# Chunk inputs in two tiles, decays loaded first, gate rows a product ahead, and a chunk's finish in a later step: one layer of a hybrid decoder on one core

## The chip, the core and the metric

The kernel runs on one core of a Trainium2 chip. The time is the device time of one execution in microseconds (us), from start to end, as the median of several runs. A trace of one further, profiled execution goes with it. The core has five engines with their own instruction streams: PE (TensorE, matmuls and transposes; PEld is its weight load), DVE (VectorE), ACT (ScalarE), POOL (GpSimd) and SP (SyncE, which here only issues DMA transfers; some are issued by ACT). The engines meet through semaphores. The granted clock is the share of full speed at which TensorE was allowed to run.

## What is computed

One layer: a pooling branch P and a state-space branch S run in parallel, are gated, added and multiplied by `w_o`. Prompt: 1 sequence of 1024 rows; sample: 8 sequences of 8 rows (64 rows, so 1088 in all). Cut to what matters here:

```python
u_pool, z_pool, z_ssm, xbc, dt_raw, g_raw = split(h @ w_in)
p = (pool_mix(u_pool) * silu(z_pool)) @ w_pool_out            # 512 -> 1024
xs, B, C = split(silu(causal_conv(xbc)))                      # 2048, 4*128, 4*128
# ssd, per chunk of 128 rows and per group g of 8 heads:
acs = cumsum(dt * A); decay = exp(where(mask, acs_i - acs_j, -inf))
y = ((C B^T) * decay * dt) @ x + (C * exp(acs)) @ h
h = h * exp(acs_last) + (B^T, exp(acs_last - acs) * dt) @ x
y = rmsnorm((y + d_skip * x) * silu(z_ssm), ssm_norm_g)
s = y @ w_ssm_out                                             # 2048 -> 1024
x = x + gate * ((sigmoid(g_p) * p + sigmoid(g_s) * s) @ w_o)
```

Outputs are the final norm of both streams and the new pool, convolution and ssm states.

## The kernel before

Each matrix operand is held as a high and a low part, and a product takes three matmuls (high by high, high by low, low by high), in helpers whose lines are L359, L360 and L361 or L608, L609 and L610. Channels lie on the partitions and rows run along the free axis.

**Three stages** can be told apart in time. To about 815 us the conditioning and the in-projection run; they leave x, B and C of the four groups (`xbc_d[g]`, six blocks of 128 channels: four of x, one of B, one of C), `silu(z)` (`z_d[g]`) and the gate rows (`gp_d`, `gs_d`) in DRAM. From 815 to 1127 us comes the **chunk stage**, which the change edits. The rest, to 1307 us, is the last group's share of the S product, the gating, the product with `w_o` and the final norm.

**The chunk stage** walks 32 chunks, 4 groups `g` of 8 chunks `c` with 128 rows each, and lays the large products between them so that PE has work while a chunk's small steps run on the other engines. `chunk(g, c)` is a generator of steps:

- step 1 loads `xb` (x, B and C of the chunk, 128x6x128, L1492, 4 buffers) and `dec` (the cumulated decays spread over partitions, 128x8x128, L1187 in `decays`, 3 buffers);
- step 2 makes `cE` from `dec` on ACT (L1499), masks `dec` on POOL (L1192) and takes its 8 exponentials on ACT (L1201, one for a head);
- step 3 loads `sz` (the chunk of `silu(z)`, L1505, 3 buffers), transposes x and B on PE (L1508, L1510) and multiplies C by B (L1511); ACT copies B and C out (L1513, L1515); DVE scales x into `xd`, `xw` (L1519, L1521) and multiplies `dec` and `cE` (L1526, L1528);
- step 4 is the matmuls `pu` (L1533) and `inner` (L1213, L1216), the new state `hn` (POOL L1539, DVE L1541) and `v`, the output with the skip term, written over x in `xb` (DVE L1546). Then follows `finish`: `v*sz` (DVE L1468), the high part `yh` (ACT L1470), the square into `sz` (ACT L1471), the low part `yl` (POOL L1472), and the sum of squares into `sq_acc` (POOL L1473 to L1479);
- for the last chunk of a group, step 5 transposes the state out through `fo` (1 buffer, L1552 to L1555).

`sample_end(g)` does the same finish for the sample's 64 rows; it takes a tile of the ring `sz` and loads it (L1483), and `v` (L1485).

**The main loop** (L1803 to L1825) runs in iteration `i`: a step of `wos`; step 3 of chunk i+1; products; step 5 of chunk i-1 if there is one; a step of `wos`; step 4 with the finish of chunk i; the sample's loads where i%8 is 2, its finish where i%8 is 4; step 1 of chunk i+3; step 2 of chunk i+2; products. `products` advances the large products at RATE 2.56 blocks an iteration: first eight P products (`P_unit`), each with a gate row `R` (128x1088) loaded from `gp_d` as it begins (L1719), multiplied by DVE (L1722) and stored by ACT (L1724); then the S products of groups 0 to 2. The weights of a product are loaded two products ahead (L459, L460). `wos` splits `w_o` into high and low parts in 16 pieces: a piece is loaded (`pw`, 2 buffers, L1772), copied to its high part on ACT (L1775), which is stored, and POOL subtracts (L1777); in its next step the low part is written back through SP (L1781).

`in_line` (L1830) puts PE's and SP's instructions in the order in which the program is written; the scheduler orders ACT, DVE and POOL, and `behind(...)` is a hint to it that holds a piece of work behind other work on an engine. SP takes its queue in order: an issue that waits for a buffer holds all issues behind it.

Of the kernel before, what the change touches and what calls it, by code (L numbers as in the profile page):

```python
# [8 lines left out]
F32 = mybir.dt.float32  # L9
# [11 lines left out]
P = 128  # L21
# [4 lines left out]
NS = 64  # L26
# [7 lines left out]
NC = SEQ // CH  # L34
# [12 lines left out]
def tile_pool_ssd_step(  # L47
# [9 lines left out]
    def nm(s):  # L57
        uid[0] += 1
        return f"{s}_{uid[0]}"
# [31 lines left out]
    def R(shape=(P, T), dt=F32):  # L91
        return hs.tile(list(shape), dt, tag="R", name=nm("R"), bufs=3)
# [17 lines left out]
    load = nc.sync.dma_start  # L110
    store_ = nc.scalar.dma_start
# [1072 lines left out]
    def decays(dec, g, c):  # L1184

        S = P if c < NC else NS
        load(dec, acs_d[c, 8 * g:8 * g + 8, :S].partition_broadcast(S))  # L1187
# [273 lines left out]
    CKL = ("sz", "v")  # L1461

    def ckt(shape, tag, bufs=2):
        return (cl if tag in CKL else ca if tag in ("dec", "xb", "cE") else ck).tile(list(shape), F32, tag=tag, name=nm(tag), bufs=bufs)

    def finish(g, o, S, v, sz):

        V.tensor_tensor(v, v, sz, ALU.mult)  # L1468
        yhc = yh[g][:, :, o:o + S]
        act(yhc, v, AF.Copy)  # L1470
        act(sz, v, AF.Square)  # L1471
        nc.gpsimd.tensor_tensor(yl[g][:, :, o:o + S], v, yhc.bitcast(F32), ALU.subtract)  # L1472
        nc.gpsimd.tensor_tensor(sz[:, 0:2], sz[:, 0:2], sz[:, 2:4], ALU.add)  # L1473
        sa = sq_acc[:, o:o + S]
        if g == 0:
            nc.gpsimd.tensor_tensor(sa, sz[:, 0], sz[:, 1], ALU.add)
# [12 lines left out]
    def chunk(g, c):  # L1489
        o = c * P  # L1490
        xb = ckt([P, 6, P], "xb", 4)
        load(xb, xbc_d[g][:, :, o:o + P])  # L1492
        Bf, Cf = xb[:, 4], xb[:, 5]
        dec = ckt([P, 8, P], "dec", 3)
        decays(dec, g, c)
        yield
        if c > 0:
            cE = ckt([P, 8, P], "cE")
            act(cE, dec, AF.Exp, scale=-1.0)  # L1499
# [5 lines left out]
        load(sz, z_d[g][:, :, o:o + P])  # L1505
        px = PB()
        for q in range(4):
            nc.tensor.transpose(px[:, q * P:(q + 1) * P], xb[:, q], ident)  # L1508
        pbc = PB()
        nc.tensor.transpose(pbc[:, :P], Bf, ident)  # L1510
        mm(pbc[:, P:2 * P], Bf, Cf, start=True, stop=True)  # L1511
        bt = ckt([P, P], "bt", 2)
        act(bt, pbc[:, :P], AF.Copy)  # L1513
        if c > 0:
            act(pbc[:, 2 * P:3 * P], Cf, AF.Copy)  # L1515
        pxv = px.rearrange("p (h d) -> p h d", d=64)
        heads = slice(8 * g, 8 * g + 8)
        xd = ckt([P, 8, 64], "xd", 2)
        V.tensor_tensor(xd, pxv, dtT[:, c, heads].unsqueeze(2).to_broadcast([P, 8, 64]), ALU.mult)  # L1519
        xw = ckt([P, 8, 64], "xw", 1)  # L1520
        V.tensor_tensor(xw, pxv, wdT[:, c, heads].unsqueeze(2).to_broadcast([P, 8, 64]), ALU.mult)  # L1521
        if g == c == 0:
            yield
            far(dec, c)
            exps(dec, g, c)
        V.tensor_tensor(dec, dec, pbc[:, P:2 * P].unsqueeze(1).to_broadcast([P, 8, P]), ALU.mult)  # L1526
        if c > 0:
            V.tensor_tensor(cE, cE, pbc[:, 2 * P:3 * P].unsqueeze(1).to_broadcast([P, 8, P]), ALU.mult)  # L1528
        yield
        if c == 0:  # L1530
            yh[g], yl[g] = [Y4(hs if g % 2 else hp) for _ in range(2)]
        pu = PC()
        mm(pu, bt, xw.rearrange("p h d -> p (h d)"), start=True, stop=True)  # L1533
        pi = inner(xd, dec, P, *((hst[g], cE) if c > 0 else ()))
        hn = ckt([P, 512], "hst", 2)
        if c == 0:
            act(hn, pu, AF.Copy)
        else:
            nc.gpsimd.tensor_tensor(hn.rearrange("p (h d) -> p h d", d=64), hst[g].rearrange("p (h d) -> p h d", d=64),  # L1539
                                    Elb[:, c, heads].unsqueeze(2).to_broadcast([P, 8, 64]), ALU.mult)  # L1540
            V.tensor_tensor(hn, hn, pu, ALU.add)  # L1541
        hst[g] = hn

        v = xb[:, 0:4]
        for q in range(4):
            V.scalar_tensor_tensor(v[:, q], v[:, q], Dv[:, 4 * g + q:4 * g + q + 1], pi[:, q], ALU.mult, ALU.add)  # L1546
        finish(g, o, P, v, sz)
        if c == NC - 1:
            yield
            pt = PB()  # L1550
            for q in range(4):
                nc.tensor.transpose(pt[:, q * P:(q + 1) * P], hn[:, q * P:(q + 1) * P], ident)  # L1552
            fo = ckt([P, 4, P], "fo", 1)
            act(fo, pt.rearrange("p (q n) -> p q n", n=P), AF.Copy)
            store_(new_ssm_p[0, 0, 8 * g:8 * g + 8].rearrange("(q h) p n -> (h p) q n", h=2), fo)  # L1555

# [154 lines left out]

    def P_unit(m):
        def run(w):
            if m == 0:
                sg = first_g[0]
            else:
                sg = R()
                with behind(mybir.EngineType.SP):
                    load(sg, gp_d[m])  # L1719

            def done(o, n, ps):
                V.tensor_tensor(sg[:, o:o + n], ps[:, :n], sg[:, o:o + n], ALU.mult)  # L1722
# [43 lines left out]

    def wo_splits():
        raws = {}
        for n in range(18):
            if n < 16:  # L1770
                raws[n] = ck.tile([P, 512], F32, tag="pw", name=nm("pw"), bufs=2)
                load(raws[n], w_o[0, n // 2 * P:n // 2 * P + P, n % 2 * 512:n % 2 * 512 + 512])  # L1772
            if 0 < n < 17:
                hi = ck.tile([P, 512], F32R, tag="ph", name=nm("ph"), bufs=1)
                act(hi, raws[n - 1], AF.Copy)  # L1775
                store_(wo_d[(n - 1) // 2][:, 0, (n - 1) % 2 * 512:(n - 1) % 2 * 512 + 512], hi.bitcast(F32))
                nc.gpsimd.tensor_tensor(raws[n - 1].bitcast(F32R), raws[n - 1], hi.bitcast(F32), ALU.subtract)  # L1777
                lo = raws.pop(n - 1)
            yield
            if 0 < n < 17:  # L1780
                load(wo_d[(n - 1) // 2][:, 1, (n - 1) % 2 * 512:(n - 1) % 2 * 512 + 512], lo)  # L1781
            yield
    wos = wo_splits()
    RATE = 2.56
# [2 lines left out]
    def products(t):  # L1787

        nonlocal made
        while made < RATE * t:  # L1790
            next(pc_, None)
            made += 1

    first_engines = (mybir.EngineType.PE, mybir.EngineType.Activation, mybir.EngineType.DVE, mybir.EngineType.SP)
    in_line(first_engines, True)
    next(seq[0])
# [3 lines left out]
    next(seq[1])  # L1800
    next(pc_)
    in_line(first_engines)
    for i in range(len(seq)):  # L1803
# [12 lines left out]
        if i % NC == 2:  # L1816
            ends = sample_end(i // NC)
            next(ends)
        if i % NC == 4:
            next(ends, None)  # L1820
        if i + 3 < len(seq):
            next(seq[i + 3])
        if i + 2 < len(seq):
            next(seq[i + 2])
        products(i + 1.0)  # L1825
    next(seq[-1], None)
    for it in (pc_, wos):
        for _ in it:
            pass
    in_line((mybir.EngineType.PE, mybir.EngineType.SP))  # L1830
    right.__exit__(None, None, None)
    while right_all:
        right_all.pop().__exit__(None, None, None)
# [223 lines left out]
```

## Time and profile before

| | us |
|---|---|
| median of 3 runs | 1303.44 |
| lowest and highest run | 1301.71, 1304.66 |
| the profiled execution's own time | 1308.79 |
| its span, first to last instruction | 1307.1 |

The mean granted clock of the profiled execution is 0.99. In 40 slices of the span (32.7 us each), a digit is the busy share of a slice in tenths; PEclk is the granted clock in tenths:

```profile
PE   7999999999999999999999999989999999999998
DVE  4685778866978688776666764666767767466433
PEclk9999999999999999999999999989999999999999
```

The chunk stage is slices 26 to 35. PE is busy nearly throughout; one slice, the 27th, about 850 to 882 us, has PE and its clock lower.

### The profile page before, as it was taken

What the parts mean: (1) busy time and instruction counts of PE and PEld (TensorE: products, weight loads), DVE (VectorE), ACT (ScalarE), POOL (GpSimd) and SP (SyncE); (2) the same over time, 40 slices, a digit from 0 to 9 for tenths busy, and PEclk for the clock granted to TensorE, in tenths of its full rate; (3) what the DMA queues carried; (4) which work ended last, traced back from release to release, by engine and by line L of the source; (5) the groups of instructions that cost most, each with busy time, mean ns of one, the idle gap of its engine ahead of it and who ended that gap; (6) DMA issues with size and microseconds to landing.
All of it is one profiled execution on the core that took longest, in us unless ns stands there. A gap on an engine that the chain in (4) does not pass through costs nothing.

```text
span 1307.1 us, 26274 instructions
## 1 busy us (share of the span) xinstructions
PE 1263.8 (97%) x9739; PEld 1174.2 (90%) x9739; DVE 899.7 (69%) x1608; ACT 662.5 (51%) x1528; POOL 669.5 (51%) x563
## 2 busy tenths in 40 slices
PE   7999999999999999999999999989999999999998
PEld 6779999999999999999999999978898788999786
DVE  4685778866978688776666764666767767466433
ACT  5665357375656564546556544545776555201211
POOL 1007668676869676665534435244676757314000
PEclk9999999999999999999999999989999999999999
DMA  9737345464455544445565656977778778575631
GB/s 333 245 110 228 112 147 184 146 204 150 153 166 197 167 152 132 160 133 143 161 206 170 180 169 221 303 248 268 226 243 271 246 244 283 198 262 158 227 101 52
DMA packets 232257, 251.68 MB, mean 193 GB/s; under 512 B 29217, under 2 KB 176369, under 8 KB 232122
## 3 DMA queue, kind: packets, MB, share of 16 engines
q1 hardware_dynamic: 160032, 171.60, 41.3%
q10 hardware_dynamic: 72098, 78.41, 17.6%
q8 instruction: 77, 1.26, 0.4%
q14 instruction: 50, 0.41, 0.1%
HBM read 167.06 MB, written 83.01 MB: 191 GB/s over the span
## 4 chain that ended last, share of the span: by engine, by line
PE 58%; issue 8%; DMA 8%; POOL 6%; DVE 4%; ACT 2%; SPq 0%; ACTq 0%; POOLq 0%; DVEq 0%
PE ps L608 6%; PE ps L609 6%; PE ps L610 6%; PE mm L608 6%; PE mm L610 6%; PE mm L609 5%; PE mm L359 3%; PE mm L360 3%; PE mm L361 3%; PE ps L2004 2%; PE ps L2003 2%; PE ps L2005 2%; PE ps L1213 2%; POOL G L1912 2%; DMA dec<-acs_d 1%
## 5 line engine op out<-in xcount | busy, mean ns | idle before, releaser
L168 POOL TENSOR_TENSOR wlo<-rawA,whi 128x512 fp32r<-128x512 f32 x120 | 179.4, 1499 | 179.6 <-ACT whi L165 104.0
L168 POOL TENSOR_TENSOR wlo<-raw,whi 128x512 fp32r<-128x512 f32 x92 | 149.9, 1636 | 122.1 <-ACT whi L165 87.5
L359 PE MATMUL mm<-Y,whi 128*128 128x352 f32 (+1 forms) x480 | 165.8, 345 | 5.6 <-DVE R L1722 4.8
L360 PE MATMUL mm<-Y,whi 128*128 128x352 f32 (+1 forms) x480 | 159.5, 332 | 0.3 <-DVE Y L1570 0.3
L361 PE MATMUL mm<-Y,wlo 128*128 128x352 f32 (+1 forms) x480 | 159.0, 331 | 0.0
L608 PE MATMUL mm<-Y,whi 128*128 128x272 f32 x496 | 146.4, 295 | 0.6 <-DVE GA L624 0.5
L610 PE MATMUL mm<-Y,wlo 128*128 128x272 f32 x496 | 144.4, 291 | 2.6 <-POOL wlo L168 2.1
L608 PE MATMUL ps<-Y,whi 128*128 128x272 f32 x496 | 144.0, 290 | 2.6 <-ACT o L808 2.2
L609 PE MATMUL ps<-Y,whi 128*128 128x272 f32 x496 | 143.6, 290 | 0.0
L610 PE MATMUL ps<-Y,wlo 128*128 128x272 f32 x496 | 143.1, 289 | 0.0
L609 PE MATMUL mm<-Y,whi 128*128 128x272 f32 x496 | 142.7, 288 | 0.0
L1056 DVE SCALAR_TENSOR_TENSOR GA<-GA,cvT,GA 128x1112 f32<-128x1112 f32 x72 | 129.0, 1795 | 1.4 <-ACT GA L1053 1.3
L165 ACT ACTIVATE whi<-rawA 128x512 fp32r<-128x512 f32 x125 | 78.3, 627 | 92.1 <-PE ps L609 47.5
L165 ACT ACTIVATE whi<-raw 128x512 fp32r<-128x512 f32 x96 | 58.9, 627 | 104.5 <-DVE raw L554 47.8
L359 PEld LDWEIGHTS mm<-Y,whi 128*128 128x128 f32 x480 | 91.8, 191 | 12.4 <-DVE R L1722 5.3
L610 PEld LDWEIGHTS mm<-Y,wlo 128*128 128x128 f32 x496 | 93.5, 189 | 4.4 <-POOL wlo L168 3.2
L608 PEld LDWEIGHTS ps<-Y,whi 128*128 128x128 f32 x496 | 93.9, 189 | 3.2 <-ACT o L808 2.5
L1201 ACT ACTIVATE dec<-dec,acT 128x128 f32<-128x128 f32 (+1 forms) x288 | 87.0, 383 | 18.3 <-POOL dec L1192 17.9
L608 PEld LDWEIGHTS mm<-Y,whi 128*128 128x128 f32 x496 | 93.3, 188 | 3.0 <-DVE GA L624 0.6
L609 PEld LDWEIGHTS mm<-Y,whi 128*128 128x128 f32 x496 | 93.6, 189 | 0.9
L610 PEld LDWEIGHTS ps<-Y,wlo 128*128 128x128 f32 x496 | 94.0, 190 | 0.0
L609 PEld LDWEIGHTS ps<-Y,whi 128*128 128x128 f32 x496 | 93.9, 189 | 0.0
(452 smaller groups left out, 3763.6 us busy)
## 6 DMA issues: line engine op xcount, KB each, us to landing
rawA<-in_w_in SPq DMA_DIRECT2D x46, 512.0 KB
dec<-acs_d SPq DMA_DIRECT2D x32, 512.0 KB
xbc<-GA ACTq DMA_DIRECT2D x24, 512.0 KB
xb<-xbc SPq DMA_DIRECT2D x32, 384.0 KB
rawA<-in_w_in SPq DMA_DIRECT2D x32, 256.0 KB
pw<-in_w_ssm_out ACTq DMA_DIRECT2D x32, 256.0 KB
ws<-ph ACTq DMA_DIRECT2D x32, 256.0 KB
ws<-pw SPq DMA_DIRECT2D x32, 256.0 KB
```

The lines of the kernel that those rows point to most:

```text
L165: ins = act(hi[:, :, :ncols], raw[:, :, :ncols], AF.Copy)
L168: (eng or nc.gpsimd).tensor_tensor(lo[:, :, :ncols], raw[:, :, :ncols], hi[:, :, :ncols].bitcast(F32), ALU.subtract)
L359: mm(ps[:, :n], a, rh[k][:, o:o + n], start=(k == 0), stop=False)
L360: mm(ps[:, :n], a, rl[k][:, o:o + n], start=False, stop=False)
L361: mm(ps[:, :n], b, rh[k][:, o:o + n], start=False, stop=(k == nk - 1))
L608: mm(p, hi, ah, start=(k == 0), stop=False)
L609: mm(p, hi, al, start=False, stop=False)
L610: mm(p, lo, ah, start=False, stop=(k == 3))
L1056: V.scalar_tensor_tensor(d[:, :n], rp[:, k:k + n], cvT[:, 24 * k + mc:24 * k + mc + 1], d[:, :n], ALU.mult, ALU.add)
L1201: act(dec[:, h], dec[:, h], AF.Exp, bias=acT[:S, c, 8 * g + h:8 * g + h + 1], scale=-1.0)
L1213: mm(o[hh], xd[:S, 2 * q + hh, :], dec[:S, 2 * q + hh], start=True, stop=state is None)
L1912: (nc.gpsimd if m < 7 else V).tensor_tensor(a[:, s], a[:, s], mt[:, s], ALU.add)
```

## The change

- `xb` is cut in two: `bc` holds B and C (128x2x128, 3 buffers) and `xb` only x (128x4x128, 5 buffers instead of 4). The order of step 1 is now `dec`, `bc`, `xb`. `v` is the whole of `xb`. `bc` joins the pool in which `dec`, `xb` and `cE` lie.
- The sample's tile has a ring of its own, `szs`, with one buffer; it no longer takes one of the three of `sz`.
- `fo` takes a buffer of the ring `xb`.
- The finish of a chunk is a step of its own. In the loop it comes after step 1 of chunk i+3 and step 2 of chunk i+2, ahead of the sample's finish, of `wos` and of the iteration's last products.
- A P product loads the gate row of the product after it, as it begins, without the hint; the first row is loaded ahead of the stage as before.
- `wos` has 3 buffers `pw` and one step an iteration, at its end: write back the low part of piece n-2, split piece n-1, load piece n. The hints around it are gone.

```diff
-        sz = ckt([P, 4, P], "sz", 3)[:, :, :NS]
+        sz = ckt([P, 4, NS], "szs", 1)
...
-        xb = ckt([P, 6, P], "xb", 4)
-        load(xb, xbc_d[g][:, :, o:o + P])
-        Bf, Cf = xb[:, 4], xb[:, 5]
         dec = ckt([P, 8, P], "dec", 3)
         decays(dec, g, c)
+        bc = ckt([P, 2, P], "bc", 3)
+        load(bc, xbc_d[g][:, 4:6, o:o + P])
+        Bf, Cf = bc[:, 0], bc[:, 1]
+        xb = ckt([P, 4, P], "xb", 5)
+        load(xb, xbc_d[g][:, 0:4, o:o + P])
...
-        v = xb[:, 0:4]
+        v = xb
...
+        yield
         finish(g, o, P, v, sz)
...
-            fo = ckt([P, 4, P], "fo", 1)
+            fo = ckt([P, 4, P], "xb", 5)
...
-            if m == 0:
-                sg = first_g[0]
-            else:
-                sg = R()
-                with behind(mybir.EngineType.SP):
-                    load(sg, gp_d[m])
+            sg = first_g.pop(0)
+            if m < 7:
+                first_g.append(R())
+                load(first_g[0], gp_d[m + 1])
...
         for n in range(18):
-            if n < 16:
-                raws[n] = ck.tile([P, 512], F32, tag="pw", name=nm("pw"), bufs=2)
-                load(raws[n], w_o[0, n // 2 * P:n // 2 * P + P, n % 2 * 512:n % 2 * 512 + 512])
+            if n > 1:
+                load(at(n - 2, 1), raws.pop(n - 2))
             if 0 < n < 17:
...
-                lo = raws.pop(n - 1)
-            yield
-            if 0 < n < 17:
-                load(wo_d[(n - 1) // 2][:, 1, (n - 1) % 2 * 512:(n - 1) % 2 * 512 + 512], lo)
+            if n < 16:
+                raws[n] = ck.tile([P, 512], F32, tag="pw", name=nm("pw"), bufs=3)
+                load(raws[n], w_o[0, n // 2 * P:n // 2 * P + P, n % 2 * 512:n % 2 * 512 + 512])
             yield
...
     for i in range(len(seq)):
-        if i > 12:
-            with behind(mybir.EngineType.Activation), behind(mybir.EngineType.SP), behind(mybir.EngineType.Pool):
-                next(wos, None)
...
-        if i > 12:
-            with behind(mybir.EngineType.Activation), behind(mybir.EngineType.SP), behind(mybir.EngineType.Pool):
-                next(wos, None)
         next(seq[i], None)
...
-        if i % NC == 4:
-            next(ends, None)
         if i + 3 < len(seq):
             next(seq[i + 3])
         if i + 2 < len(seq):
             next(seq[i + 2])
+        next(seq[i], None)
+        if i % NC == 4:
+            next(ends, None)
+        if i > 12:
+            next(wos, None)
         products(i + 1.0)
```

No arithmetic is added or taken away. PE's instructions keep their order; only names differ. SP has 492 rows before and 524 after, the 32 more being the loads of `bc`. Three places of the order follow. A row names the line, the kind, the output and the input with its shape.

**SP, early in the stage.** From step 1 in iteration 1 (chunk 4) to step 1 in iteration 2 (chunk 5); `R` is the gate row, `whi` and `wlo` are weights. Before:

```order
L1492 DMA xb_1918_11502<-xbc0_170 128x6x128
L1187 DMA dec_1919_11504<-acs_d_138 128x1024
L459 DMA whi_1922_11534<-wp5_183 128x512
L460 DMA wlo_1923_11535<-wp5_183 128x512
L1719 DMA R_1924_11538<-gp3_153 128x1088
L1505 DMA sz_1926_11554<-z0_166 128x4x128
L1483 DMA sz_1936_11619<-z0_166 128x4x64
L1485 DMA v_1937_11621<-ys0_174 128x256
L1492 DMA xb_1938_11623<-xbc0_170 128x6x128
```

Now:

```order
L1187 DMA dec_1923_11506<-acs_d_138 128x1024
L1494 DMA bc_1924_11508<-xbc0_170 128x2x128
L1497 DMA xb_1925_11510<-xbc0_170 128x4x128
L459 DMA whi_1928_11546<-wp5_183 128x512
L460 DMA wlo_1929_11547<-wp5_183 128x512
L1720 DMA R_1930_11550<-gp4_154 128x1088
L1507 DMA sz_1932_11566<-z0_166 128x4x128
L1483 DMA szs_1942_11625<-z0_166 128x4x64
L1485 DMA v_1943_11627<-ys0_174 128x256
L1187 DMA dec_1944_11629<-acs_d_138 128x1024
```

The row `R` at this place is that of `gp4` instead of `gp3`, `dec` has moved ahead of x, B and C, and the sample's load writes `szs`.

**SP, the pieces of `w_o`.** The brackets name what an issue waits for: `DMAHW0` to `DMAHW7` are eight semaphores that the program gives to its DMAs in turn, so that a DMA waits until the one eight before it has landed; the others are the engines that used the buffer last. Before, one iteration and the start of the next:

```order
L1492 DMA xb_2248_13529<-xbc2_172 128x6x128 [waits DMAHW6_49,DVE_49,Activation_49]
L1187 DMA dec_2249_13531<-acs_d_138 128x1024 [waits DMAHW7_49,PE_49]
L459 DMA whi_2251_13546<-ws14_198 128x512 [waits DMAHW0_49]
L460 DMA wlo_2252_13547<-ws14_198 128x512 [waits DMAHW1_49]
L1772 DMA pw_2255_13578<-in_w_o 128x512 [waits DMAHW5_49,DMAHW2_49]
L1505 DMA sz_2257_13584<-z2_168 128x4x128 [waits DMAHW3_49,Pool_49]
L1781 DMA wo3_11214<-pw_2236_13456 128x512 [waits Pool_49]
L1492 DMA xb_2267_13658<-xbc2_172 128x6x128 [waits DMAHW6_49,DVE_49,Activation_49]
L1187 DMA dec_2268_13660<-acs_d_138 128x1024 [waits DMAHW7_49,PE_49]
```

Now:

```order
L1187 DMA dec_2288_13682<-acs_d_138 128x1024 [waits DMAHW2_49,DVE_49,PE_49]
L1494 DMA bc_2289_13684<-xbc2_172 128x2x128 [waits DMAHW3_49,Activation_49]
L1497 DMA xb_2290_13686<-xbc2_172 128x4x128 [waits DMAHW4_49]
L1775 DMA wo2_11219<-pw_2256_13483 128x512 [waits DMAHW5_49]
L1783 DMA pw_2293_13720<-in_w_o 128x512 [waits DMAHW6_49]
L459 DMA whi_2294_13722<-ws15_199 128x512 [waits DMAHW7_49]
L460 DMA wlo_2295_13723<-ws15_199 128x512 [waits DMAHW0_49]
L1507 DMA sz_2297_13740<-z2_168 128x4x128 [waits DMAHW1_49,Activation_49,Pool_49]
L1187 DMA dec_2307_13799<-acs_d_138 128x1024 [waits DMAHW2_49,DVE_49,PE_49]
```

The iteration begins with `dec` instead of `xb`. `xb` and the write-back of the low part wait for no engine any more, only for a transfer; `pw` waits for one transfer instead of two. With the store of the high part, which ACT issues, the eight semaphores went round once in an iteration, `xb` always on the same one; now it takes nine.

**ACT, the finish of an early chunk.** `Y` is `yh`, `sz` the square, `dec` the exponentials of a later chunk. Before, the finish stands after the second of the eight exponentials; the rest follow it:

```order
L1201 ACTIVATE dec_11504<-dec_11504,acT 128x128 x2
L1470 ACTIVATE Y_11374<-xb_11133 128x4x128
L1471 ACTIVATE sz_11437<-xb_11133 128x512
L1201 ACTIVATE dec_11504<-dec_11504,acT 128x128 x6
L1515 ACTIVATE ps_11661<-xb_11502 128x128
```

Now:

```order
L1201 ACTIVATE dec_11506<-dec_11506,acT 128x128 x8
L1470 ACTIVATE Y_11382<-xb_11141 128x4x128
L1471 ACTIVATE sz_11447<-xb_11141 128x512
L1517 ACTIVATE ps_11675<-bc_11508 128x128
```

The finish has moved behind all eight exponentials of the chunk two ahead. Elsewhere on ACT, DVE and POOL neighbouring rows change places in the same manner.

More of the change, by code (lines that the diff above doesn't have):

```diff
@@ L1463, in ckt @@
     def ckt(shape, tag, bufs=2):
-        return (cl if tag in CKL else ca if tag in ("dec", "xb", "cE") else ck).tile(list(shape), F32, tag=tag, name=nm(tag), bufs=bufs)
+        return (cl if tag in CKL else ca if tag in ("dec", "xb", "cE", "bc") else ck).tile(list(shape), F32, tag=tag, name=nm(tag), bufs=bufs)
     def finish(g, o, S, v, sz):
@@ L1768, in wo_splits, with at @@
         raws = {}
+        def at(n, t):
+            return wo_d[n // 2][:, t, n % 2 * 512:n % 2 * 512 + 512]
         for n in range(18):
-            if n < 16:
-                raws[n] = ck.tile([P, 512], F32, tag="pw", name=nm("pw"), bufs=2)
-                load(raws[n], w_o[0, n // 2 * P:n // 2 * P + P, n % 2 * 512:n % 2 * 512 + 512])
+            if n > 1:
+                load(at(n - 2, 1), raws.pop(n - 2))
             if 0 < n < 17:
@@ L1775, in wo_splits @@
                 act(hi, raws[n - 1], AF.Copy)
-                store_(wo_d[(n - 1) // 2][:, 0, (n - 1) % 2 * 512:(n - 1) % 2 * 512 + 512], hi.bitcast(F32))
+                store_(at(n - 1, 0), hi.bitcast(F32))
                 nc.gpsimd.tensor_tensor(raws[n - 1].bitcast(F32R), raws[n - 1], hi.bitcast(F32), ALU.subtract)
-                lo = raws.pop(n - 1)
-            yield
-            if 0 < n < 17:
-                load(wo_d[(n - 1) // 2][:, 1, (n - 1) % 2 * 512:(n - 1) % 2 * 512 + 512], lo)
+            if n < 16:
+                raws[n] = ck.tile([P, 512], F32, tag="pw", name=nm("pw"), bufs=3)
+                load(raws[n], w_o[0, n // 2 * P:n // 2 * P + P, n % 2 * 512:n % 2 * 512 + 512])
             yield
@@ L1792, in products @@
             made += 1
+    ORDER = ("PE","SP")
     first_engines = (mybir.EngineType.PE, mybir.EngineType.Activation, mybir.EngineType.DVE, mybir.EngineType.SP)
@@ L1802, in tile_pool_ssd_step @@
     in_line(first_engines)
+    order = tuple(mybir.EngineType[e] for e in ORDER)
     for i in range(len(seq)):
-        if i > 12:
-            with behind(mybir.EngineType.Activation), behind(mybir.EngineType.SP), behind(mybir.EngineType.Pool):
-                next(wos, None)
         if i + 1 < len(seq):
@@ L1829, in tile_pool_ssd_step @@
             pass
-    in_line((mybir.EngineType.PE, mybir.EngineType.SP))
+    in_line(order)
     right.__exit__(None, None, None)
```

## The prediction

> **What bounds the kernel now.** I read the page's engine totals first, then a view by windows cut at the three stages. Its columns are the window's length, then busy time and instructions of PE, PEld, DVE, ACT and POOL, the granted clock, the DMA engines' busy share and GB/s.
>
> ```profile
> PE 1263.8 (97%) x9739; PEld 1174.2 (90%) x9739; DVE 899.7 (69%) x1608; ACT 662.5 (51%) x1528; POOL 669.5 (51%) x563
> ...
> 815.00:1127.00 312.00, 297.31 (x2327) 263.61 (x2325) 219.02 (x383) 179.93 (x467) 178.93 (x206) 0.98 0.77 253
> ```
>
> PE bounds the kernel at 97%, so a change that leaves PE's work and order alone can win only what PE idles and what its clock loses. In the chunk stage, the only one edited, PE idles 312.0 − 297.3 = 14.7 us, and 2% of 312 us, about 6 us, is the clock. Next, the waits of PE in that stage (total, times, longest):
>
> ```profile
> PE ps L1508 <- DMA xb<-xbc: 5.4, 2, 2.8
> PE mm L359 <- DVE R L1722: 4.8, 1, 4.8
> PE ps L1510 <- DVE cE L1528: 2.6, 3, 1.3
> PE ps L1508 <- ACT fo L1554: 1.6, 1, 1.6
> ```
>
> So nearly all the idle time, 5.4 + 4.8 + 2.6 + 1.6 = 14.4 us, lies in seven waits. Last, the clock in 20 us windows around the large ones:
>
> ```profile
> 870.00:890.00 20.00, 19.66 (x138) 17.06 (x139) 15.10 (x27) 8.94 (x23) 9.04 (x10) 0.85 0.69 232
> 1010.00:1030.00 20.00, 17.16 (x141) 14.99 (x141) 14.39 (x27) 9.46 (x26) 12.85 (x17) 1.00 0.63 198
> 1050.00:1070.00 20.00, 17.17 (x130) 14.73 (x130) 12.33 (x20) 12.42 (x30) 11.05 (x14) 1.00 0.96 314
> 1070.00:1090.00 20.00, 17.40 (x130) 15.43 (x130) 13.07 (x26) 9.67 (x27) 12.91 (x14) 0.91 0.49 161
> ```
>
> The clock falls to 0.85 behind the 4.8 us wait and to 0.91 behind the second wait for `xb`: 20 × 0.15 + 20 × 0.09 = 4.8 us. The whole stage's 0.98 would give 6.2; I take 4.8, the two rows. The most that is there to win is therefore 14.4 + 4.8 = 19.2 us.
>
> **Where the waits come from, and what the change does to each.** The chain of waits and SP's timeline (start, duration) lead from a late landing back to its issue. The gate row first:
>
> ```profile
> 860.47 0.33 POOL sq_acc L1476
> 860.79 0.02 issue
> 860.81 0.52 SPq L1505
> ...
> 862.51 7.19 DMA R<-gp
> ...
> 869.72 0.57 DVE R L1722
> ...
> 870.34 0.69 PE mm L359
> ```
>
> ```profile
> 852.38 0.59 SPq L1187 DMA_DIRECT2D dec<-acs_d  x1
> 860.81 0.52 SPq L1505 DMA_DIRECT2D sz<-z  x1
> ```
>
> SP issued `dec` at 852.4 and then nothing for 8.4 us: `sz` had to wait for a finish, because the sample had taken one of the three `sz` buffers. The weights and the gate row stood behind it. The row, issued at 862.5, took 7.2 us, and PE stood at a full product until DVE had read it. Two edits remove this, either alone: the gate row now goes out with the product before, at three blocks a product and 2.56 blocks an iteration some 11 us sooner (3 / 2.56 × 312 / 32), against the wait of 4.8; and `szs` leaves `sz` its third buffer. The new row needs a third `R` while its predecessor is in use and the one before that is being stored; there are three. This term is 4.8 us of idle and 3.0 of clock: **7.8**.
>
> The first late `xb`:
>
> ```profile
> 1005.78 0.38 SPq L1772 DMA_DIRECT2D pw<-in_w_o  x1
> 1016.27 0.52 SPq L1505 DMA_DIRECT2D sz<-z  x1
> 1016.85 0.61 SPq L1781 DMA_DIRECT2D wo<-pw  x1
> 1017.56 0.52 SPq L1492 DMA_DIRECT2D xb<-xbc  x1
> ```
>
> ```profile
> 1017.56 6.17 DMA xb<-xbc
> 1023.73 0.14 issue
> 1023.86 0.63 PE ps L1508 x4
> ```
>
> Again SP stands at `sz` (10.5 us), again just after a sample took a buffer, and `xb` goes out behind it. With `szs` and a fifth `xb` this goes: 2.8, no clock. The second late `xb`:
>
> ```profile
> 1066.21 0.39 SPq L1781 DMA_DIRECT2D wo<-pw  x1
> 1079.61 0.53 SPq L1492 DMA_DIRECT2D xb<-xbc  x1
> ...
> 1078.30 1.30 POOL Y L1472
> 1079.61 3.67 DMA xb<-xbc
> ```
>
> SP is held 13.4 us by `xb` itself, until POOL has read the chunk four before; that finish was late because, by the program, the last group's `yh` reuses memory that the products of group 1 still read. Five buffers ask for the chunk five before, a whole iteration (9.75 us) earlier, and `xb` no longer stands ahead of `dec`. The wait after it is 2.6 us; its clock 1.8: **2.8 + 2.6 + 1.8 = 7.2**.
>
> The late `dec`:
>
> ```profile
> 1048.81 0.52 SPq L1492 DMA_DIRECT2D xb<-xbc  x1
> 1050.89 0.32 SPq L1187 DMA_DIRECT2D dec<-acs_d  x1
> 1055.62 0.33 SPq L1772 DMA_DIRECT2D pw<-in_w_o  x1
> ...
> 1050.89 7.08 DMA dec<-acs_d
> ```
>
> `dec` landed at 1058.0; ACT's `cE`, its copies and DVE's L1528 followed, and PE lost 2.6 us in three small waits. The 1.6 us put down to `fo` lie in the same stretch, on the same late ACT. Now `dec` is issued where `xb` was, 1050.89 − 1048.81 = 2.1 us sooner. That does not cover 2.6 + 1.6 = 4.2; I count **2.7** and leave 1.5 standing. ACT waits for this transfer often, so the margin is small everywhere:
>
> ```profile
> ACT cE L1499 <- DMA dec<-acs_d: 33.9, 14, 6.2
> SPq L1187 <- DMA dec<-acs_d: 2.3, 2, 1.5
> SPq L1781 <- POOL pw L1777: 38.8, 9, 6.0
> ```
>
> **The rest of the edits.** SP's largest wait, 38.8 us at the write-back of a low part, goes, since that is issued an iteration after its subtraction; it was no term of its own, as its blocked time shows up in the late `dec` and `xb`. Its move behind `xb` puts it ahead of `pw` and the weights, both loaded over an iteration ahead. The finish moves behind the exponentials and the mask of the chunk two ahead:
>
> ```profile
> L1201 ACT ACTIVATE dec<-dec,acT 128x128 f32<-128x128 f32 (+1 forms) x288 | 87.0, 383 | 18.3 <-POOL dec L1192 17.9
> ```
>
> That is up to 8 × 0.383 = 3.1 us on ACT. Nothing on PE reads `yh` within the iteration; who waits is `sz` three chunks on (SP) and, behind it, the loads. What hides the 3.1 us is the two iterations, 19 us, between that finish and the `sz` that wants its buffer; without that cover SP would hand on up to 3.1 us a chunk. I take nothing. In return the `dec`, the next thing on PE's path, is masked and exponentiated sooner.
>
> The 32 loads of `bc` are 32 more issues, 0.52 us each by the rows of `xb`: 17 us if SP were the bound, nothing while SP stands still for 8 to 13 us at a time. What counts is that they take a place among the eight semaphores that go round: an iteration with a piece of `w_o` took eight transfers and takes nine, so a transfer may wait for one that is an issue younger. Its bounds are nothing and, by the row of `dec` waiting for an older transfer, 1.5 us in each of the 19 chunks beside `w_o`, 28 us; the row's total of 2.3 us in a whole stage is nearest, and I take 2.5 with any other new small wait. The **sum** is 7.8 + 7.2 + 2.7 = 17.7, less 2.5 = 15.2 us. The profiled execution's own time is 1308.79, 5.35 above the median of the runs shown: 1308.8 − 15.2 = 1293.6 there, 1293.6 − 5.35 = 1288.2 as a median. I predict **1288 us**.
>
> The Trainium skill, "TensorE: Matmul & The Clock Gate", in "HAM oscillation — how this bites in real kernels", says: "The abstract rule is "no PE-idle gaps >~3.4µs."" By it only the 4.8 us gap would cost clock and that term would be 3.0, the sum 13.4; the trace agrees for the 4.8 us gap and for the 2.8 us one (1.00), but the 2.6 us gap has 0.91 behind it, so the measurement decides and both are counted.
>
> **Rivals.** *The waits move to `dec` and the transfers.* The DMA engines are 0.96 busy around 1050, ACT waits for `dec` 14 times, and no byte fewer is moved. Then only the gate row's 7.8 us come for good and the late part's 9.6 us of idle return under other names: 1303.4 − 7.8 = **1296**. Against it: two of the late landings follow SP's standing still at 0.63 and 0.49 DMA share, not a time of full transfer engines.
>
> *It does not do what it says.* If `sz` still holds SP where it did (its finish is now later), a gate row ahead and a fifth `xb` stand in the same queue and land as late: **1303**. For it: SP's order is fixed, and one held issue holds all. Against: `sz` has all three buffers now.
>
> *Slower: the eight semaphores become the bound.* With nine transfers of mean flight F in an iteration and eight places, an iteration beside `w_o` takes at least 9F/8. That decides from F = 8.1 us (9.15 us an iteration, which is (312 − 19.2) / 32), and the whole comes out 2.6 us slower when 19 such iterations of 9F/8 − 9.75 eat the 7.8 of the gate row and 2.6 more: F = 9.2. At 9.5 it is 19 × 0.94 − 7.8 = 10 us slower, **1313**. The flights shown above, 3.67 to 7.19 us, speak against it, and the halves of a transfer should not fly longer than the whole. For it speak the 0.96 of DMA share at 1050 and the longest flight in the chain, another gate row's, which lies between the two bounds:
>
> ```profile
> 843.52 8.36 DMA R<-gp
> ```
>
> [...]
>
> **How the numbers follow.** Forecast 0.62, its own range 1281 to 1294; the waits move, 0.20 (1294 to 1299); no change, 0.08; slower, 0.10. 0.2%, 2.6 us, is about what a measurement here can tell from no change. Faster by more: 0.62 + 0.20 = 0.82; same 0.08; slower 0.10. The lower end: all 14.4 and the larger 6.2 of the clock with no charge gives 1303.4 − 20.6 = 1282.8, and the runs shown scatter by 1.5 either way: 1281. The upper end takes in the first rival and most of the second: 1304. Left out are the slower case and a few hundredths at each end, under 0.2.
>
> **What would show it.** In the changed profile PE's wait at L359 for the gate row is gone and no window of the stage has a clock below 0.95; the wait for `xb` at the transposes is gone and SP no longer stands at the `sz` load for 8 us after a sample; a little waiting behind `cE` remains; PE's idle time in the stage falls from 14.7 us to about 4. Wrong would be a new PE wait of 3 us or more behind `dec`, `bc` or `sz`, flights above 8 us between 950 and 1127, or an SP that waits for transfers to land.

## The result, and the profile after

The changed kernel takes **1286.74 us** (median of 4 runs, 1286.20 to 1287.28) against 1304.05 us before (4 runs, 1301.71 to 1310.71): a ratio of 0.9859, 95% interval 0.9823 to 0.9896. The forecast was 1288 us within 1281 to 1304.

The profiled execution took 1286.55 us. Its page opens like this, engine totals as in the prediction:

```profile
span 1284.8 us, 26305 instructions
...
PE 1256.1 (98%) x9739; PEld 1169.3 (91%) x9739; DVE 897.6 (70%) x1608; ACT 662.2 (52%) x1528; POOL 670.9 (52%) x563
```

Every engine does the same work; the span is 22.3 us shorter. The waits of PE in the chunk stage, seven that came to 14.4 us before, are now these, of which the second was there before too:

```profile
PE ps L1512 <- DVE cE L1530: 1.1, 1, 1.1
PE mm L360 <- DVE Y L1573: 0.3, 1, 0.3
```

The view by windows (columns as in the prediction). First the window before that held the gate row's wait:

```profile
850.00:870.00 20.00, 14.76 (x129) 13.16 (x128) 12.87 (x23) 9.19 (x25) 8.85 (x11) 0.98 0.75 248
```

Now the changed kernel: the stage, which ends 20.4 us sooner, the same window, and the one behind it, whose clock was 0.85:

```profile
815.00:1106.60 291.60, 290.26 (x2316) 258.81 (x2314) 219.83 (x382) 179.45 (x467) 179.15 (x206) 1.00 0.85 269
850.00:870.00 20.00, 20.00 (x167) 17.91 (x164) 16.10 (x31) 11.55 (x29) 12.62 (x15) 1.00 1.00 314
870.00:890.00 20.00, 20.00 (x162) 18.08 (x161) 16.51 (x31) 11.16 (x33) 9.35 (x11) 1.00 0.92 289
```

PE idles 291.6 − 290.3 = 1.3 us there instead of 14.7, and the granted clock is 1.00. In the window 850 to 870, in which the gate row was waited for, PE is busy throughout, and the share of the transfer engines is 1.00 instead of 0.75.

Since PE executes the same instructions in the same order, its 9739 matmuls can be set beside each other one by one; such a comparison is called matched below. These are the places in the stage where the lead of the changed kernel grows or shrinks by over 0.5 us (start in the execution before, step in us, line before):

```text
 855.36  +0.97  L1510
 870.34  +7.74  L359   gate row: 4.8 of wait, the rest clock
 917.65  +0.80  L1510
1003.90  -1.27  L1510  the one wait that is new
1023.86  +3.03  L1508  first late xb
1059.79  +1.78  L1508
1061.72  +1.49  L1510  both behind the late dec
1083.42  +2.79  L1508  second late xb
1084.47  +1.56  L360   clock behind it
```

These come to 18.9 us. Another 1.4 us is gained ahead of 815 us and 1.9 us behind 1127 us, where nothing was edited.

What SP does with its time has changed too. Its main waits between 800 and 1115 us:

```profile
SPq L1187 <- PE ps L1216: 85.6, 24, 6.7
SPq L1507 <- DMA wo<-ph: 14.0, 5, 5.0
...
SPq L1507 <- POOL sq_acc L1479: 8.9, 3, 5.7
```

SP now mostly stands at `dec`, at the head of an iteration, for its buffer, which PE's `inner` frees: SP is ahead of the work. It also waits for landings, the longest in total at `sz` for the store of a high part (`ph`), which ACT issues. Before, it stood at the write-back of a low part (38.8 us, shown in the prediction), at `sz` and at `xb`, with other loads behind them. The rows for `xb`, of the view from 815 to 1130 us:

```profile
SPq L1492 <- ACT sz L1471: 28.2, 8, 5.2
SPq L1492 <- POOL Y L1472: 21.4, 11, 12.9
```

### The profile page after: what moved, and what is told of

It reads as the page before. It is cut to its first block, busy times and chain, and to the rows that moved or that the text cites. A ratio compares the mean times of both kernels' runs of the same rounds, so it can differ in the third digit from the quotient of the medians.

```text
span 1284.8 us, 26305 instructions
## 1 busy us (share of the span) xinstructions
PE 1256.1 (98%) x9739; PEld 1169.3 (91%) x9739; DVE 897.6 (70%) x1608; ACT 662.2 (52%) x1528; POOL 670.9 (52%) x563
## 4 chain that ended last, share of the span: by engine, by line
PE 63%; issue 7%; DMA 7%; POOL 4%; ACT 2%; DVE 2%; SPq 0%; ACTq 0%; POOLq 0%; DVEq 0%
PE ps L608 6%; PE ps L609 5%; PE ps L610 5%; PE mm L608 5%; PE mm L610 5%; PE mm L609 5%; PE mm L359 4%; PE mm L360 4%; PE mm L361 4%; PE ps L1213 3%; PE ps L2004 2%; PE ps L2006 2%; PE ps L2005 2%; PE pc L1535 2%; PE ps L1216 2%
## 5 line engine op out<-in xcount | busy, mean ns | idle before, releaser
L359 PE MATMUL mm<-Y,whi 128*128 128x352 f32 (+1 forms) x480 | 163.5, 341 | 0.6 <-DVE G L1907 0.5
L360 PE MATMUL mm<-Y,whi 128*128 128x352 f32 (+1 forms) x480 | 157.4, 328 | 0.3 <-DVE Y L1573 0.3
L359 PEld LDWEIGHTS mm<-Y,whi 128*128 128x128 f32 x480 | 90.2, 188 | 7.1 <-issue 4.8
```

The lines of the kernel that those rows point to most:

```text
L359: mm(ps[:, :n], a, rh[k][:, o:o + n], start=(k == 0), stop=False)
L360: mm(ps[:, :n], a, rl[k][:, o:o + n], start=False, stop=False)
```

## The experiments

Each was timed beside the kernel before on the same chip; its medians there were 1303.8 to 1304.1 us. The changed kernel itself was not run again beside them, and the runs of one kernel scatter by up to 4 us (1284.27 to 1288.48 in one case below), so a difference of 1 or 2 us between two medians is not a finding by itself. The theory: PE's waits come from SP's queue, held by one issue, and the edits take the holds away, the gate row ahead and the sample's own tile for the first, the rest for the later ones. The rivals are the prediction's: the transfers or the eight semaphores bind, or the edits do not do what they say.

**The kernel before, profiled again.**

> The kernel before, profiled a second time. Matched instruction by instruction, the profiled execution of the changed kernel is 22.3 us shorter than that of before, while the medians differ by 16 to 17 us, and the profiled execution of before lay 5.35 us above its median. Theory: the same seven waits of PE come again, 14 us give or take 2, and what varies between executions is the clock behind them, so this profile has a span nearer to 1302 us with a mean clock above 0.990. Rival: the waits themselves differ from execution to execution; then some of the seven are missing or half as long.

It took 1307.33 us (span 1305.6, mean clock 0.993). PE's waits:

```profile
PE mm L359 <- DVE R L1722: 6.2, 2, 6.0
PE ps L1508 <- DMA xb<-xbc: 5.3, 2, 2.8
PE ps L1510 <- DVE cE L1528: 3.5, 3, 1.3
PE ps L1508 <- ACT fo L1554: 1.4, 1, 1.4
```

The same waits at the same places, 16.4 us against 14.4: they belong to the kernel and not to one execution. The other half of the theory fell: the span is not near 1302. The two profiled executions of before, 1308.79 and 1307.33, both lie 3 to 5 us above its median, and matched against the changed kernel the second gives 20.8 us, where the medians give 17.3.

**The gate row and the sample's tile: each undone alone, and both.**

```diff
-            sg = first_g.pop(0)
-            if m < 7:
-                first_g.append(R())
-                load(first_g[0], gp_d[m + 1])
+            if m == 0:
+                sg = first_g[0]
+            else:
+                sg = R()
+                load(sg, gp_d[m])
```

> The changed kernel, but each P product loads its own gate row as it begins, without the hint. The prediction said that the gate row ahead and the sample's own tile each remove the wait alone: then no wait for R at L359 of more than 1 us and a time within 1.5 us of the changed kernel, 1285 to 1288.5. Rival: the row's flight of 7 to 8 us is longer than what a product gives it, whoever holds SP; then the wait for R comes back with 3 to 5 us and the clock behind it, 1291 to 1296.

1287.66 us (1286.25 to 1289.05), ratio 0.9869 (0.9854 to 0.9884); the only wait for the gate row at L359 is 0.8 us.

```diff
-        sz = ckt([P, 4, NS], "szs", 1)
+        sz = ckt([P, 4, P], "sz", 3)[:, :, :NS]
```

> The changed kernel, but the sample takes a tile of the ring sz again. Theory: SP stands at the sz load after each sample as before (a wait of 8 to 10 us), yet the gate row is a product ahead and xb has five buffers, so PE sees little: 1286 to 1289, no wait above 1.5 us. Rival: SP's standing still is the cause and the other edits only move it; then a late dec or xb costs 3 us or more behind the samples of groups 1 to 3, 1290 to 1296.

1286.85 us (1284.27 to 1288.48), ratio 0.9856 (0.9837 to 0.9875); PE's longest wait in the stage is 0.7 us. SP's longest wait at `sz` is 5.7 us, shorter than the 8 to 10 expected.

> Both of these undone at once. Theory: the gate row is late again behind the held sz load, the wait of 4 to 6 us at L359 comes back and about 3 us of clock with it: 7.8 us, 1293 to 1296. Rival: with dec ahead and the finish moved SP is held at another place and the row lands in time: below 1289.

1293.60 us (1292.91 to 1295.62), ratio 0.9917 (0.9902 to 0.9932). The wait is back, and the chain of waits and SP's timeline read as before:

```profile
PE mm L359 <- DVE R L1724: 4.9, 2, 4.4
```

```profile
861.01 0.34 POOL sq_acc L1476
...
863.08 5.61 DMA R<-gp
```

```profile
852.66 0.46 SPq L1497 DMA_DIRECT2D xb<-xbc  x1
861.37 0.53 SPq L1507 DMA_DIRECT2D sz<-z  x1
```

From `xb` to `sz` SP lets 8.7 us pass, until POOL has done `sq_acc`; the gate row leaves at 863 and PE waits. Either edit alone removes it, as predicted; both undone cost 1293.60 − 1286.74 = 6.9 us. The rival that the flight alone is too long fell with the first run.

**Four edits of the later part, each undone.** `dec` behind `bc` and `xb`:

> The changed kernel, but step 1 loads bc, xb, dec in this order. Theory, as in the prediction: dec leaves two issues later, about 1 us, half of the late dec comes back as small waits behind cE: 1287.5 to 1289.5. Rival: in the changed kernel SP stands at dec until its buffer is free (85.6 us in 24 waits), so bc and xb ahead of it cost dec nothing: 1286 to 1287.5 and no new wait. Second rival: dec is what the late part hangs on, all of 2.7 and more comes back: 1290 or above.

1287.03 us (1286.20 to 1290.08), ratio 0.9867 (0.9844 to 0.9891). Its trace has one wait of 1.1 us, at the transposes for `cE`, at another chunk than the changed kernel's own (1045 us), and no other above 0.3. The first rival holds as to the time: SP is ahead, and two issues in front of `dec` cost nothing that can be measured.

The finish with its `v`, in one step (the `yield` ahead of it and the third `next(seq[i], None)` taken out):

> The changed kernel, but the finish of a chunk follows its v at once again, ahead of the masks and exponentials of the chunk two ahead. Theory, as in the prediction: the move neither costs nor brings anything that can be measured, 1285.5 to 1288.5. Rival: the move is what makes the exponentials early enough, so undoing it brings back waits of PE behind cE or dec of 3 us or more, 1289 to 1293.

1285.33 us (1282.56 to 1285.62), ratio 0.9844 (0.9818 to 0.9870): 1.4 us below the changed kernel and just below the theory's range; the intervals of the ratios overlap, the runs of the two kernels do not. The rival, waits of 3 us or more, fell. Its trace has PE waits of 0.3 us in all; matched with the changed kernel, its gain in the stage is 1.2 us at one place, the wait for `cE` that was new. That wait in the changed kernel, and what ACT does ahead of it:

```profile
994.15 0.30 PE L1512 MATMUL ps<-ident,bc 128*128 128x128 f32 x1 [1.08 <-DVE cE L1530]
```

```profile
987.98 0.25 ACT L1515 ACTIVATE bt<-ps 128x128 f32<-128x128 f32 x1
990.65 0.63 ACT L1778 ACTIVATE ph<-pw 128x512 fp32r<-128x512 f32 x1 [2.42 <-DMA pw<-in_w_o]
991.19 0.26 ACT L1517 ACTIVATE ps<-bc 128x128 f32<-128x128 f32 x1
```

The same place with the finish back:

```profile
985.28 0.26 ACT L1515 ACTIVATE bt<-ps 128x128 f32<-128x128 f32 x1
986.49 0.63 ACT L1777 ACTIVATE ph<-pw 128x512 fp32r<-128x512 f32 x1 [0.95 <-DMA pw<-in_w_o]
987.03 0.26 ACT L1517 ACTIVATE ps<-bc 128x128 f32<-128x128 f32 x1
```

ACT's order is the same in both here, and the finish stands ahead of the exponentials in both (at 984.6 and 981.9). Between the copies of B and of C stands a side load: ACT copies a piece of `w_o` (`ph`) and waits for it to land, 2.42 us against 0.95, and DVE waits for C before it makes `cE`. By issue and landing in the traces this piece flew 7.9 us in the changed kernel and 5.4 with the finish back. With the sample in the ring `sz` it flew 7.5, and PE waited 0.7 us at this place; in five other runs of this section, which all keep the moved finish, it flew 4.5 to 6.6 us and PE did not wait here. So this wait comes from the late piece, and not from the move. Nor does the rest of the 1.4 us point to the finish: the profiled execution with the finish back was 1.8 us ahead at 815 us already, before the stage begins.

Four buffers `xb`, `fo` with a tile of its own:

> The changed kernel with four buffers xb and fo in a tile of its own. Theory, as in the prediction: SP stands for the xb of chunk 29 until late again, but dec is ahead of it now; PE waits 1.5 to 3 us for xb near the end of group 3 with up to 1.8 us of clock: 1288 to 1291. Rival: since xb waits for no engine at most places any more, the ring of five is idle: 1286 to 1287.5.

1287.11 us (1286.29 to 1288.64), ratio 0.9865 (0.9844 to 0.9886). The trace has two waits for `xb`, 1.9 us in all and 2.2 matched, and no clock behind them. So the waits came as the theory has them; but this execution does not have the changed kernel's wait at `cE`, and the median is 0.4 us above, within the scatter, below the theory's 1288 to 1291.

The splitting of `w_o` as before:

```diff
-                raws[n] = ck.tile([P, 512], F32, tag="pw", name=nm("pw"), bufs=3)
+                raws[n] = ck.tile([P, 512], F32, tag="pw", name=nm("pw"), bufs=2)
...
-            if n > 1:
-                load(at(n - 2, 1), raws.pop(n - 2))
...
+            yield
+            if 0 < n < 17:
+                load(wo_d[(n - 1) // 2][:, 1, (n - 1) % 2 * 512:(n - 1) % 2 * 512 + 512], lo)
             yield
```

> The changed kernel with the splitting of w_o as before: two buffers, two steps an iteration, the low part written back half an iteration after its subtraction, with the hints. Theory, as in the prediction: SP stands 30 to 40 us at the write-back in all, and that shows as a late dec or xb of 1 to 3 us for PE: 1288 to 1290. Rival: with sz free and xb deep enough it shows nowhere, 1286 to 1287.5. Second rival: it is the main cause of the late part, 1292 or above.

1297.72 us (1296.23 to 1298.78), ratio 0.9944 (0.9923 to 0.9966): **11.0 us** above the changed kernel, the second rival. PE waits for `xb` three times, and SP at the write-back of the low part (L1782):

```profile
PE ps L1510 <- DMA xb<-xbc: 7.8, 3, 2.8
```

```profile
SPq L1782 <- POOL pw L1778: 51.5, 12, 9.3
```

The first of the three in SP's timeline and the chain:

```profile
995.24 0.53 SPq L1507 DMA_DIRECT2D sz<-z  x1
1005.19 0.34 SPq L1782 DMA_DIRECT2D wo<-pw  x1
1005.63 0.37 SPq L1187 DMA_DIRECT2D dec<-acs_d  x1
...
1006.56 0.46 SPq L1497 DMA_DIRECT2D xb<-xbc  x1
```

```profile
1006.56 5.64 DMA xb<-xbc
...
1012.33 0.63 PE ps L1510 x4
```

From `sz` to the next issue SP lets 9.9 us pass, and that issue is the write-back of a low part, for which POOL had to subtract first. `dec`, `bc` and `xb` wait behind it, however many buffers they have. The other two waits follow write-backs issued at 1041.71 and 1090.02 us in the same way.

**Parts of the change alone, and the write-back moved.** The kernel before with the new splitting of `w_o` and nothing else:

> The kernel before with only the new splitting of w_o (three buffers, one step an iteration, the low part written back a step after its subtraction). The undoing of it cost 11 us. Theory: SP's standing at the write-back of the low part is what made xb and dec late from 1000 us on, so both waits for xb, and those behind dec, go and the gate row's wait stays: 1293 to 1297. Rival: the sample's tile in the ring sz and the four xb hold SP just as long without it, and the pieces matter only beside the other edits: 1299 to 1304.

1302.56 us (10 runs, 1299.47 to 1305.04), ratio 0.9989 (0.9976 to 1.0002), not told apart from the kernel before: the theory's time fell and the rival held. The waits for `xb` did go, to 0.3 us, but another of 4.4 us came. SP's hold has moved on to the head of its queue, where `xb` stands with four buffers:

```profile
PE ps L1508 <- ACT dec L1201: 4.4, 1, 4.4
```

```profile
SPq L1492 <- ACT sz L1471: 49.2, 15, 5.9
SPq L1492 <- POOL Y L1472: 32.8, 18, 15.5
```

With the gate row ahead as well:

> The kernel before with two of the edits alone: the gate row a product ahead, and the new splitting of w_o. xb is whole with four buffers and ahead of dec, the sample shares sz, the finish stands where it was. Theory: these two carry the change, the others are worth 0 to 2 us together: 1285 to 1290. Rival: the split of xb and the order of the loads carry a third of it: 1291 to 1296.

1295.32 us (1292.39 to 1295.87), ratio 0.9933 (0.9918 to 0.9948). The gate row is worth 1302.56 − 1295.32 = 7.2 us here, and the other edits together 1295.32 − 1286.74 = 8.6, not 0 to 2. The time lies in the rival's range; which of the edits carry the 8.6 is not told apart. One wait of PE, 4.9 us at the transposes, holds most of it with its clock (7.8 us matched). The chain ahead of it, and POOL's mask of the chunk whose exponentials PE waits for:

```profile
1040.39 0.52 SPq L1492
...
1041.01 0.58 SPq L1187
...
1042.12 5.42 DMA pw<-in_w_o
...
1047.64 0.07 ACT ph L1775
...
1048.98 2.15 ACT dec L1201 x7
...
1051.14 1.09 PE ps L1508 x4
```

```profile
1047.34 1.09 POOL L1192 TENSOR_SCALAR_AFFINE_SELECT dec<-dec 128x1024 f32<-128x1024 f32 x1 [2.96 <-ACT cE L1499]
```

SP stood at `xb`, so `dec` (L1187) and the piece of `w_o` behind it were issued late. The chain names the piece, which landed last: ACT's copy of it, and the copy of C behind that, stood ahead of the exponentials to 1048.4. But the mask of the late `dec` ended at 1048.4 as well, so `dec` alone would have held them as long. What the piece adds is about 0.2 us at most.

The changed kernel with the low part written back in the step in which it is subtracted:

```diff
-            if n > 1:
-                load(at(n - 2, 1), raws.pop(n - 2))
...
                 nc.gpsimd.tensor_tensor(raws[n - 1].bitcast(F32R), raws[n - 1], hi.bitcast(F32), ALU.subtract)
+                load(at(n - 1, 1), raws.pop(n - 1))
```

> The changed kernel, but the low part of a piece is written back in the step in which it is subtracted, not a step later; three buffers and one step an iteration stay. Theory: the write-back waits for ACT's copy and POOL's subtraction with the rest of SP's queue behind it, so xb and dec are late as with the old splitting: 1293 to 1299. Rival: the delay is not the point, the third buffer and the hints' absence are: 1286 to 1289.

1285.37 us (1283.59 to 1285.62), ratio 0.9862 (0.9845 to 0.9878). The rival's first half held: the delay is not the point. SP does wait at the write-back, 19.8 us in nine waits of 4.9 at most, but look at what stands around one of them:

```profile
997.22 0.46 SPq L1497 DMA_DIRECT2D xb<-xbc  x1
999.15 0.33 SPq L1779 DMA_DIRECT2D wo<-pw  x1
999.53 0.42 SPq L1782 DMA_DIRECT2D pw<-in_w_o  x1
```

The three loads of a chunk are out already; only a piece of `w_o` and then weights wait behind it. Whether the place at the end of the iteration, the third buffer or the hints' absence does more was not tried apart.

**More transfers.** `xb` in four transfers:

```diff
-        load(xb, xbc_d[g][:, 0:4, o:o + P])
+        for q in range(4):
+            load(xb[:, q:q + 1], xbc_d[g][:, q:q + 1, o:o + P])
```

> The changed kernel with xb loaded by four transfers of 64 KB instead of one of 256 KB: twelve transfers in an iteration beside w_o instead of nine, with the same bytes. The slower rival of the prediction is that the eight semaphores in turn become the bound: with flights of 6.5 us an iteration would take 12 x 6.5 / 8 = 9.75 us against 9.15, 0.6 x 19 = 11 us more, 1295 to 1300. Theory: the smaller transfers land sooner and SP is far enough ahead: 1286 to 1289.

1296.08 us (1292.72 to 1298.34), ratio 0.9941 (0.9922 to 0.9960): 9.3 us above the changed kernel for the same bytes. PE has five waits behind `cE` and `dec`, 6.6 us in all, and SP waits for landings where it stood at `dec` for a buffer (20.3 us now, 85.6 in the changed kernel):

```profile
PE ps L1511 <- DVE cE L1531: 2.9, 1, 2.9
```

```profile
SPq L1784 <- DMA wo<-ph: 21.2, 9, 5.2
SPq L1187 <- PE ps L1216: 20.3, 8, 3.9
...
SPq L1776 <- DMA sz<-z: 7.6, 5, 2.2
```

So with twelve transfers in an iteration the eight semaphores hold SP, and PE feels it; with nine, SP waits for landings too, and PE loses 1.3 us at one place. That the loss is near the 11 us of the rival's sum is luck, though. The sum takes flights of 6.5 us; by the issues and landings in the trace from 950 to 1110 us they last 5.1 us on average, and with these it gives 12 x 5.1 / 8 = 7.7 us, less than an iteration of 9.1 us (291.6 / 32), and so no loss. The holds come unevenly, up to 5.2 us for a single transfer and most of all for the store that ACT issues, and most of the loss lies at three places, not in every iteration. That a smaller transfer, or the three more issues of SP, also has a cost of its own is not told apart here.

## Why the prediction was right, and where it was not

**The bound was right.** PE alone bounds the stage; the gain is PE's idle time and the clock behind it, and of the 14.7 us that PE idled 1.3 are left. The signs that the prediction named came: no wait at L359, no wait for `xb`, no window of the stage below 0.95 in clock, a little waiting behind `cE`. Two of its signs of being wrong came as well: SP waits for transfers to land (14.0 us at `sz`), and two flights reach 8.2 us by the landings in the trace, both issued at 983 to 984 us. In the same burst of issues went the late piece of `w_o`, behind which PE has its one new wait, 1.1 us.

**The terms**, as predicted and as the matched matmuls of the first profile have them: gate row 7.8, measured 0.97 + 7.74 = 8.7; both late `xb` with the clock 7.2, measured 3.03 + 2.79 + 1.56 = 7.4; late `dec` 2.7, measured 1.78 + 1.49 = 3.3; the charge for new waits 2.5, measured 1.27. With 0.80 at 917.65 us the stage gives 18.9, not 15.2. The prediction misread one row here: it put all three waits for `cE`, 2.6 us, into the stretch of the late `dec`, but by the matched matmuls they lie at 855, 917 and 1062 us, and only the last, 1.3 us, is in that stretch. The first hangs on the gate row before, the 8.36 us flight. So of the 1.5 us that it left standing as `dec`'s, nearly all was not `dec`'s, and went too. The caution, those 1.5 and the charge of 2.5, was too large.

**The step from the profiled execution to the median was wrong.** It carried the 5.35 us by which the profile of before lay above its median over to the changed kernel. That kernel's profile lies within its other runs, 1286.55 among 1286.20 to 1287.28: nothing was to be subtracted. So a sum 7 us short of the 22.3 that the profiles differ by, and a subtraction of 5.35, nearly cancel, and 1288 is closer than its working deserves. Of the surplus 3.3 us lay outside the stage; the second profile of before had its surplus without them. What lengthens the profiled executions of before stays open; other runs of that kernel also reach 1307 to 1311 us, and in the eleven experiments with several runs the profiled one lies from 1.8 us below its median to 1.6 above.

**What removes which wait was partly wrong.** For the gate row the reading was right in full: either edit is enough (1287.66, 1286.85), neither costs 6.9. For the late `xb` and `dec` the prediction named `szs`, the fifth buffer and the order of the loads, and said of the splitting of `w_o` that SP's 38.8 us "was no term of its own, as its blocked time shows up in the late `dec` and `xb`". That step failed: undone one by one, the three named are worth 0.1, 0.4 and 0.3 us in the medians, not told apart from nothing (only the fifth buffer shows in a trace, by 1.9 us of waits), and the splitting 11.0. Alone the splitting is worth 1.4, not told apart from nothing either. So no single edit owns the 10 us of the late part: SP's queue had several places at which it was held, at `xb`, at `sz` and at the write-back. With the write-back alone left as it was, it holds the loads behind it; with the write-back alone cured, SP is held at `xb`. The smaller edits seem to cover for each other: singly they cost next to nothing, and without all of them, the new splitting and the early gate row in place, 8.6 us are missing. The cut of `xb` in two and the finish are among the 8.6, and pairs were not tried.

**The finish was costed at nothing** with the argument that nothing on PE reads `yh`, and no run shows a cost. With the finish back the median is 1.4 us lower, but the one wait of PE that went with it hangs on a late piece of `w_o`, with ACT's order there the same in both. What the move itself costs or brings stays open, within some 1.5 us.

**The slower rival** did not come: with nine transfers in an iteration, whose flights from 950 to 1100 us average 5.6 us and reach 8.2, its rule gives 9 x 5.6 / 8 = 6.3 us, within an iteration. Twelve do cost 9.3 us, and by waits of SP for landings, but unevenly and not by that rule.

The kernels with the finish back (1285.33) and with the early write-back (1285.37) are each 1.4 us below the changed kernel in the median. No run here joins them, and their intervals overlap with its own; both profiled executions were 1.5 to 1.8 us ahead at 815 us already, before the stage begins.

## What to carry to other kernels

An in-order queue that is held at one place holds whatever stands behind it, so read a late landing back to its issue, and from there to the row before the gap; then take away all the holds on that path, since removing one can move the wait to the next. Put write-backs of side work behind the loads that the bound engine needs: behind them a wait of SP cost nothing here, ahead of them, in the old splitting, 11 us. A profiled execution's distance from the median is not to be carried over to the changed kernel. And before a wait is put down to an edit, look whether runs that keep the edit have the wait too, at the same matmul.

## What the runs showed of the hardware

The granted clock falls where nothing waits, too. The window 1140 to 1160 us of the first profile of before, then of the second:

```profile
1140.00:1160.00 20.00, 20.00 (x124) 19.97 (x124) 8.16 (x22) 0.41 (x2) 0.00 (x0) 0.91 0.77 283
```

```profile
1140.00:1160.00 20.00, 20.00 (x134) 19.97 (x133) 9.92 (x25) 0.41 (x2) 0.00 (x0) 1.00 0.78 276
```

PE is busy all 20 us in both, at the same work, and one has the clock at 0.91 and ten matmuls fewer. Matched, such a drop costs 1.56 us, here as behind the second late `xb`; it comes in one execution of this kernel and not in the other. So whether the wait of 2.6 us brought the drop behind it, as the prediction had it, is not shown, though both profiles of before have it there. A difference of 1.5 us between two single profiles may be no more than that.
